# A hybrid decoder trunk on one core: weights split one unit less ahead in attention and the delta rule, and the norm factor of the last two heads applied without a pinned step

## The chip, the cores and the metric

The kernel runs on one core of a Trainium2 chip. The metric is device time in microseconds (us) of one execution. Five engines work side by side, each with a queue of its own that it goes through in order: PE (TensorE, matmul), DVE (VectorE), ACT (ScalarE), POOL (GpSimd) and SP (SyncE, which issues nearly all DMAs here). An instruction that waits for a semaphore holds up everything behind it in its own queue.

## The reference

Two layers of a decoder block over 512 tokens of width 1024, all in float32:

```python
def hybrid_layer(x, ...):
    h = rmsnorm(x, pre_mix_g)
    proj = h @ w_in              # q|k|v|z|beta|decay of DeltaNet, q|k|v of attention, gates A|B
    y_a = deltanet_branch(...) @ w_up_dn      # causal conv + silu, gated delta rule, gated RMSNorm
    y_b = swa_sink_branch(...) @ w_up_sw      # sliding window attention with sinks
    mix = (sigmoid(gate_a) * y_a + sigmoid(gate_b) * y_b) @ w_o
    x = x + rmsnorm(mix, post_mix_g)
    h2 = rmsnorm(x, pre_mlp_g)
    ff = square(relu(h2 @ w_ff1)) @ w_ff2     # width 4096
    return x + rmsnorm(ff, post_mlp_g)

# end of deltanet_branch, o being the output of the delta rule:
    o = rmsnorm(o, norm_g) * silu(z)
```

The DeltaNet branch has 8 heads of 128. In each, with the decay g summed over the tokens of a chunk, a triangular matrix is inverted and the state passes from chunk to chunk. Attention has 16 query heads and 2 key heads of 64, blocks of 128 tokens, each block looking at itself and the one before. The norm of a head's output is one factor for each token: the RMSNorm over the head's 128 values.

## The kernel before

**Weights.** They lie in device memory as units of 128 x 1024 float32, in the order of use. `load` (L312) brings a unit into a tile `wr`, of which there are WR = 6. `prefetch` (L411) splits it: ACT copies it to `wh`, rounded to the matmul's fp32r type (L419), and DVE subtracts that from `wr` to get the remainder `wl` (L420). There are LOOK = 4 tiles of each. The left operand is split the same way into a high and a low part, and a product is three matmuls: wh by high (L435), wh by low (L436), wl by high (L437). One unit is 24 matmuls of 128 x 512. `weights` (L424) hands out unit i, and calls `prefetch(i + LOOK)` first: at the place in the program where unit i is used, the splits of all units up to i + 3 have been written.

**Order.** The kernel is written as a trace in program order. The tile framework then puts each engine's instructions in order by that place in the program and by what is ready when, so a line that is written later may come later in its queue, or may not. Two things pin an order by hand: `Order` ties all instructions of an engine that are traced between `begin` and `end` to the order of the trace, and `tc.keep_in_program_order` ties one instruction behind the one that its engine was given before it.

**Stages of a layer.** First the norm, keys and values of attention, and its queries, 8 units, stored to a scratch area `qd`. Then attention: a loop of 16 passes (L1124 to L1146). The list MIX gives each pass projections of the shared input h: K is `k_unit` (a DeltaNet head's keys, their triangle `uu`, stored to `ud`), G is `gb_unit` (a part of gate B), A is `ga_early` (a part of gate A). Each pass also starts one attention group (t, g, e): block t, key head g, one parity e of the query heads.

- `att_q` loads a group's queries `qT` through SP (L1032), one pass ahead.
- `att_group` makes the scores `ps_s` on PE (L1055), the masked scores `M`, their maximum `nm` and the sinks' part `es` on DVE, the exponentials and the normalisation on ACT (L1073, L1079); a pass or two later PE transposes them to `ps_pt`, and they are split into a high and a low part `pf`; POOL makes a masked copy `pc` of each (L1095); PE multiplies by the values into `ps_o` (L1102). `att_prep`, once per block, also makes the block's keys `kT_h` on ACT (L1024).
- The decay of DeltaNet's heads 4 to 7 comes in the same loop, in `k_unit` (that of heads 0 to 3 beside the attention queries): `decay_load` brings a tile `D` from `gd` through SP (L817), `decay_of` masks it on POOL (L821), ACT takes its last column's exponential `egl` (L823) and four exponentials of the tile (L825), and it is stored to `dd`. Its four buffers (T[5]) are shared with `uu` and others in turn, so a load of D waits until what stood there has been read for the last time, by the store to `ud` for instance.

Then V, Q and Z of the first head, the 8 units of attention's up-projection, beside which `solve` inverts the triangles on DVE, and the delta rule over 8 heads: `d_dense` (V, Q and Z projections of the next head), `d_inverse`, `d_chain` (the state from chunk to chunk), and the output's norm in `d_tail`. The last gate units `ga_unit` follow, then `yT` (the heads' outputs, split), DeltaNet's up-projection, the merge with the gates, the out projection and the MLP.

**`d_tail`** (L1292) is a generator that `d_step` moves on by one step: the sum of squares goes to memory (`sd`); it comes back as `ff`, POOL raises it to -1/2 and stores it to `fd`; `fb` is loaded from there, spread over the partitions (L1307); and DVE multiplies the head's output `yf` by it (L1309), pinned in program order. A `yield` stands between the steps, so each one is written at another place in the program: for heads 5, 6 and 7 between the gate units (L1419) and behind them (L1420).

Of the kernel before, what the change touches and what calls it, by code (L numbers as in the profile page):

```python
# [15 lines left out]
ALU = mybir.AluOpType  # L16
# [9 lines left out]
H = 8  # L26
# [17 lines left out]
LOOK = 4  # L44
# [99 lines left out]
def hybrid_trunk(ctx, tc, x, positions, pre_mix_g, dn_conv_w, dn_a_log, dn_dt_bias, dn_norm_g,  # L144
                 sw_sinks, post_mix_g, pre_mlp_g, post_mlp_g, wpk, out, depth=2, dump=None):
    nc = tc.nc
    x = x.rearrange("b s d -> (b s) d")
    out = out.rearrange("b s d -> (b s) d")
# [12 lines left out]
    tt, ts = nc.vector.tensor_tensor, nc.vector.tensor_scalar  # L161
# [21 lines left out]
    def PS(name):  # L183
        return pp.tile([P, 512], F32, name=name, tag="ps")
# [127 lines left out]
    def load(key):  # L312

        wr = wp.tile([P, 1024], F32, name="wr", bufs=WR)
        w = width(key[4])
        dma(wr[:, :w], wpk[index[key], :, :w])
        return wr

    def width(n_):
        return 512 if n_ < 0 else n_ if n_ > 512 else 2 * n_ if n_ else 1024  # L320

    def blocks(a, n_):
        k = 4 if n_ < 0 else n_ // NB if n_ > 512 else 2 if n_ else 8
        return a[:, :width(n_)].rearrange("p (k c) -> p k c", k=k)
# [82 lines left out]
            specs.append((tuple(key), key[4]))  # L407
    pre = []
    used = [0]

    def prefetch(n, wr=None, sub=tt):  # L411
        while len(pre) < min(n, len(specs)):
            src, n_ = specs[len(pre)]
            if wr is None:
                wr = src() if callable(src) else load(src)
            wh = wp.tile([P, 1024], F32R, name="wh", bufs=LOOK)
            wl = wp.tile([P, 1024], F32R, name="wl", bufs=LOOK)
            w = width(n_)
            nc.scalar.copy(wh[:, :w], wr[:, :w])  # L419
            sub(out=wl[:, :w], in0=wr[:, :w], in1=wh[:, :w].bitcast(F32), op=ALU.subtract)  # L420
            pre.append((blocks(wh, n_), blocks(wl, n_)))
            wr = None

    def weights():  # L424
        i = used[0]
        used[0] += 1
        prefetch(i + LOOK)
        r, pre[i] = pre[i], None
        return r

    def mm_a(ps, aT, ks=range(KT), w=None):
        wh, wl = w = w or weights()
        for k in ks:
            hi, lo = aT[k]
            mm(ps, lhsT=wh[:, k, :], rhs=hi, start=k == 0, stop=False)  # L435
            mm(ps, lhsT=wh[:, k, :], rhs=lo, start=False, stop=False)  # L436
            mm(ps, lhsT=wl[:, k, :], rhs=hi, start=False, stop=k == KT - 1)  # L437
        return w
# [54 lines left out]
    def mm_b4(pss, aT, then=lambda: None, onto=False):  # L493

        for j in range(4):
            if j == 2:
                then()
            wh, wl = weights()
            for t in range(NT):
                tsl = slice(t * P, (t + 1) * P)  # L500
                for r in range(2):
                    hi, lo = aT[j * 2 + r]
                    k = j * 2 + r
                    mm(pss[t], lhsT=hi[:, tsl], rhs=wh[:, r, :], start=k == 0 and not onto, stop=False,  # L504
                       skip_group_check=onto)
                    mm(pss[t], lhsT=hi[:, tsl], rhs=wl[:, r, :], start=False, stop=False,  # L506
                       skip_group_check=onto)
                    mm(pss[t], lhsT=lo[:, tsl], rhs=wh[:, r, :], start=False, stop=k == KT - 1,  # L508
                       skip_group_check=onto)

    def mm_c(pss, left, onto=False, js=range(2)):

        for j in js:
            wh, wl = weights()
            hi, lo = left[j]
            for t in range(2):
                for r in range(2):
                    c = slice(r * 256 + t * P, r * 256 + (t + 1) * P)
                    first, last = j + r == 0 and not onto, j + r == 2
                    mm(pss[t], lhsT=hi[:, c], rhs=wh[:, r, :], start=first, stop=False,  # L520
                       skip_group_check=onto)
                    mm(pss[t], lhsT=hi[:, c], rhs=wl[:, r, :], start=False, stop=False,
                       skip_group_check=onto)
                    mm(pss[t], lhsT=lo[:, c], rhs=wh[:, r, :], start=False, stop=last,
                       skip_group_check=onto)
# [14 lines left out]
    def split(src, hi, lo, sign=1.0):  # L540
        if sign < 0:
            act(out=hi, in_=src, func=AF.Copy, scale=-1.0)
            stt(out=lo, in0=src, scalar=-1.0, in1=hi.bitcast(F32), op0=ALU.mult, op1=ALU.subtract)
            return
        nc.scalar.copy(hi, src)
        tt(out=lo, in0=src, in1=hi.bitcast(F32), op=ALU.subtract)  # L546

    def pair(U, name):
        return U(name + "_h", F32R), U(name + "_l", F32R)
# [100 lines left out]
    for l in range(depth):  # L650
# [68 lines left out]
        else:  # L719
# [16 lines left out]
            mm_a2(qf0, hT, 1, wq0)  # L736
            order.end()

        cwr = T[6]("cwr")
        dma(cwr[:96, :P], dn_conv_w[l].rearrange("k (m p) -> (k m) p", p=P))  # L740
        ps = PS("ps_cw")
# [26 lines left out]
        for t in range(NT):  # L768
# [11 lines left out]
           in1=dtb.unsqueeze(2).broadcast_to([P, H, NC]), op=ALU.add)  # L780
# [509 lines left out]
        def d_tail(h):  # L1290

            w, y1 = dn.pop(("t", h))  # L1292
            wh, wl = pair(T[5], "w")
            split(w, wh, wl)
            ps = PS("ps_w")
            mm(ps, lhsT=ones_r, rhs=wh, start=True, stop=False)
            mm(ps, lhsT=ones_r, rhs=wl, start=False, stop=True)
            nc.scalar.copy(w[0:1], ps[0:1])
            dma(sd[h:h + 1, :], w[0:1])
            yield  # L1300
            ff = sm.tile([P, NC], F32, name="ff")
            dma(ff, sd[h, :].rearrange("(p j) -> p j", p=P))
            ptt(out=ff, in0=ff, in1=mhalf, op=ALU.pow)
            pdma(fd[h, :].rearrange("(p j) -> p j", p=P), ff)
            yield
            fb = T[6]("fb")
            dma(fb, fd[h, :].partition_broadcast(P))  # L1307
            yield
            tc.keep_in_program_order(tt(out=y1, in0=y1, in1=fb, op=ALU.mult))  # L1309

        tails = [d_tail(h) for h in range(H)]

        def d_step(*hs):
            for h in hs:
                if 0 <= h < H:
                    next(tails[h], None)
# [100 lines left out]
        for m in range(NA2, KT):  # L1417
            ga_unit(m)
            d_step(H - 1, H - 2, H - 3)  # L1419
        d_step(H - 1)  # L1420
        yT = []
        for k in range(KT):
            p_ = pair(T[4 + k % 4], "yT")
# [360 lines left out]
```

## Time and profile before

| | |
|---|---|
| median of 3 runs | 1816.69 us (1814.89 to 1816.76) |
| the profiled execution | 1817.76 us around a span of 1816.1 us |
| TensorE clock granted in it | 0.998 |
| DMA | 294.33 MB, mean 162 GB/s |
| chain that ended last | PE 80%, DVE 8%, ACT 6%, DMA 3%, issue 2%, POOL 1% |
| costliest groups | split of weights: ACT `wh` 372.7 us in 366, DVE `wl` 435.4 us in 366 |

The span runs from the first instruction to the last in one execution on the chip, as the hardware profiler saw it; the execution's own time holds 1.66 us more. Busy times of engines are sums over the span. In the rows of the timeline the first column is the time from the start of the span in us, the second how long the instruction was at work, then the engine, the line, the operation and its tiles, how many alike were put together (x4), and in brackets how long the engine had waited just ahead of it and for whom. In the rows of the waits stand the waiting instruction, whom it waited for, the sum in us, the count and the mean. An SPq row is SP handing a DMA to its queue: the data land later. Lines are those of the kernel before; the two layers are the same program, so that each place in layer 0 has a twin in layer 1, 896.5 us later.

### The profile page before, as it was taken

Reading aid. Unit: us, or ns where it says so; the run is one execution under the profiler, and the core shown is the slowest. Engines: PE = TensorE matmul, PEld = TensorE weight load, DVE = VectorE, ACT = ScalarE, POOL = GpSimd, SP = SyncE. Lnnn points to the kernel's source line nnn. Section 1 sums busy time; section 2 is a strip of 40 time slices with the busy share of each in tenths; the row PEclk is TensorE's granted clock in tenths of the full one; section 3 lists DMA queues with packets and bytes.
Section 4 is the critical chain, followed back from the end, with each engine's and each line's share of the span. In section 5 each row is a group of like instructions: output and inputs, shape, how many; then the busy total and the mean of one; then the engine's idle time right before and its main releaser. Section 6 shows DMA issues by size and latency. Waiting matters only on the chain.

```text
span 1816.1 us, 28412 instructions
## 1 busy us (share of the span) xinstructions
PE 1787.7 (98%) x10220; PEld 1511.2 (83%) x10220; DVE 1376.8 (76%) x2576; ACT 998.8 (55%) x2039; POOL 200.3 (11%) x346
## 2 busy tenths in 40 slices
PE   9999999999999999999999999999999999999998
PEld 7887878887788888989888877888877888889896
DVE  6489796888666878888565897878884669698973
ACT  7578732444434656566555887234443347566572
POOL 2013202221101000000020131022111010000000
PEclk9999999999999999999999999999999999999999
DMA  6845447555453255554557453575554533555551
GB/s 221 276 142 184 117 139 232 169 163 152 128 190 135 82 163 153 173 179 147 185 182 239 156 169 105 170 231 162 159 139 148 167 116 104 175 164 161 174 178 55
DMA packets 167071, 294.33 MB, mean 162 GB/s; under 512 B 34497, under 2 KB 83969, under 8 KB 166930
## 3 DMA queue, kind: packets, MB, share of 16 engines
q1 hardware_dynamic: 166418, 292.48, 51.9%
q8 instruction: 80, 1.31, 0.3%
q14 instruction: 61, 0.50, 0.1%
q0 software_dynamic: 512, 0.03, 0.0%
HBM read 246.19 MB, written 46.27 MB: 161 GB/s over the span
## 4 chain that ended last, share of the span: by engine, by line
PE 80%; DVE 8%; ACT 6%; DMA 3%; issue 2%; POOL 1%; SPq 0%; DVEq 0%; POOLq 0%; ACTq 0%
PE ps_f L435 2%; PE ps_f L436 2%; PE ps_f L437 2%; PE ps_zp L435 2%; PE ps_zp L436 2%; PE ps_b L506 2%; PE ps_us L436 2%; PE ps_b L504 2%; PE ps_b L508 2%; PE ps_us L437 2%; PE ps_us L435 2%; PE ps_zp L437 2%; PE ps_ud L436 1%; PE ps_qp L435 1%; PE ps_qp L436 1%
## 5 line engine op out<-in xcount | busy, mean ns | idle before, releaser
L419 ACT CAST wh<-wr 128x1024 fp32r<-128x1024 f32 (+2 forms) x366 | 372.7, 1023 | 416.1 <-PE ps_us L436 62.7
L420 DVE TENSOR_TENSOR wl<-wr,wh 128x1024 fp32r<-128x1024 f32 (+2 forms) x366 | 435.4, 1196 | 170.3 <-ACT wh L419 164.4
L571 POOL TENSOR_TENSOR pr<-pq,pw 128x1 f32<-128x1 f32 x16 | 9.8, 615 | 787.6 <-DVE pq L570 787.6
L435 PE MATMUL ps_f<-g_h,wh 128*128 128x512 f32 x160 | 62.4, 390 | 0.0
L436 PE MATMUL ps_f<-g_l,wh 128*128 128x512 f32 x160 | 62.4, 390 | 0.0
L437 PE MATMUL ps_f<-g_h,wl 128*128 128x512 f32 x160 | 62.2, 389 | 0.0
L1073 ACT ACTIVATE M<-M,nm 128x128 f32<-128x128 f32 x128 | 49.8, 390 | 10.9 <-DVE nm L1068 10.8
L436 PE MATMUL ps_ud<-yT_l,wh 128*128 128x512 f32 x128 | 50.7, 396 | 2.9 <-DVE yT_l L546 2.9
L435 PE MATMUL ps_zp<-h_h,wh 128*128 128x512 f32 x128 | 50.5, 394 | 2.8 <-DVE vv L883 2.8
L436 PE MATMUL ps_qp<-h_l,wh 128*128 128x512 f32 x128 | 53.2, 415 | 0.0
L437 PE MATMUL ps_qp<-h_h,wl 128*128 128x512 f32 x128 | 53.1, 415 | 0.0
L435 PE MATMUL ps_vp<-h_h,wh 128*128 128x512 f32 x128 | 52.8, 413 | 0.0
L437 PE MATMUL ps_vp<-h_h,wl 128*128 128x512 f32 x128 | 52.6, 411 | 0.0
L435 PE MATMUL ps_qp<-h_h,wh 128*128 128x512 f32 x128 | 52.5, 410 | 0.0
L435 PE MATMUL ps_ga<-h_h,wh 128*128 128x512 f32 x128 | 51.4, 402 | 1.0 <-ACT sga L946 1.0
L378 DVE TENSOR_TENSOR wr<-wr 128x512 f32<-128x512 f32 x72 | 47.5, 685 | 6.0 <-DMA wr<-in_weights_dram 5.5
L435 PE MATMUL ps_kp<-h_h,wh 128*128 128x512 f32 x128 | 51.5, 403 | 0.0
L436 PE MATMUL ps_vp<-h_l,wh 128*128 128x512 f32 x128 | 51.2, 400 | 0.0
L435 PE MATMUL ps_gb<-h_h,wh 128*128 128x512 f32 x128 | 51.2, 400 | 0.0
L437 PE MATMUL ps_ga<-h_h,wl 128*128 128x512 f32 x128 | 50.5, 395 | 0.0
L437 PE MATMUL ps_ud<-yT_h,wl 128*128 128x512 f32 x128 | 50.5, 395 | 0.0
L436 PE MATMUL ps_ga<-h_l,wh 128*128 128x512 f32 x128 | 50.5, 394 | 0.0
(449 smaller groups left out, 5958.3 us busy)
## 6 DMA issues: line engine op xcount, KB each, us to landing
wr<-in_weights_dram SPq DMA_DIRECT2D x336, 512.0 KB, 3.7
qT<-qd SPq DMA_DIRECT2D x32, 256.0 KB, 3.5
D<-dd SPq DMA_DIRECT2D x24, 256.0 KB, 2.8
xd<-xo SPq DMA_DIRECT2D x12, 512.0 KB, 2.6
xt<-xd SPq DMA_DIRECT2D x24, 256.0 KB, 6.1
qd<-qf_h SPq DMA_DIRECT2D x16, 256.0 KB, 4.2
qd<-qf_l SPq DMA_DIRECT2D x16, 256.0 KB, 3.4
D<-gd SPq DMA_DIRECT2D x16, 256.0 KB, 4.2
```

Of the source, the lines that this page charges most:

```text
L378: tt(out=o_, in0=i0, in1=i1, op=ALU.add)
L419: nc.scalar.copy(wh[:, :w], wr[:, :w])
L420: sub(out=wl[:, :w], in0=wr[:, :w], in1=wh[:, :w].bitcast(F32), op=ALU.subtract)
L435: mm(ps, lhsT=wh[:, k, :], rhs=hi, start=k == 0, stop=False)
L436: mm(ps, lhsT=wh[:, k, :], rhs=lo, start=False, stop=False)
L437: mm(ps, lhsT=wl[:, k, :], rhs=hi, start=False, stop=k == KT - 1)
L504: mm(pss[t], lhsT=hi[:, tsl], rhs=wh[:, r, :], start=k == 0 and not onto, stop=False, skip_group_check=onto)
L506: mm(pss[t], lhsT=hi[:, tsl], rhs=wl[:, r, :], start=False, stop=False, skip_group_check=onto)
L508: mm(pss[t], lhsT=lo[:, tsl], rhs=wh[:, r, :], start=False, stop=k == KT - 1, skip_group_check=onto)
L571: ptt(out=r, in0=q1, in1=mhalf[:, 0:1], op=ALU.pow)
L1073: act(out=M[:, j * P:(j + 1) * P], in_=M[:, j * P:(j + 1) * P], func=AF.Exp, bias=nm[:, j:j + 1], accum_out=den[:, j:j + 1])
```

## The change

There are two parts.

Between the end of the first attention query projection and the end of the delta rule of each layer, `weights` now calls `prefetch(i + 3)` where it called `prefetch(i + 4)`: at the place where unit i is used, splits up to unit i + 2 have been written. From `yT` on it is 4 again. The number of buffers stays: 6 `wr`, 4 `wh`, 4 `wl`. No split, load or matmul is added or dropped.

In `d_tail`, for heads 6 and 7 alone, the `yield` between the load of `fb` and the multiplication goes, and so does the pin: the multiplication is written in the same step as the load, one step earlier, and its place in DVE's queue is left to the framework.

```diff
@@ -407,6 +407,7 @@
     pre = []
     used = [0]
+    ahead = [LOOK]
 
@@ -424,7 +425,7 @@
     def weights():
         i = used[0]
         used[0] += 1
-        prefetch(i + LOOK)
+        prefetch(i + ahead[0])
         r, pre[i] = pre[i], None
         return r
 
@@ -736,6 +737,7 @@
             mm_a2(qf0, hT, 1, wq0)
             order.end()
 
+        ahead[0] = LOOK - 1
         cwr = T[6]("cwr")
@@ -1305,8 +1307,11 @@
             yield
             fb = T[6]("fb")
             dma(fb, fd[h, :].partition_broadcast(P))
-            yield
-            tc.keep_in_program_order(tt(out=y1, in0=y1, in1=fb, op=ALU.mult))
+            if h < H - 2:
+                yield
+            m_ = tt(out=y1, in0=y1, in1=fb, op=ALU.mult)
+            if h < H - 2:
+                tc.keep_in_program_order(m_)
 
@@ -1418,6 +1423,7 @@
             ga_unit(m)
             d_step(H - 1, H - 2, H - 3)
         d_step(H - 1)
+        ahead[0] = LOOK
         yT = []
```

The change writes lines in another order, so each engine's queue may come out otherwise. Rows of these queues stand in the prediction, before and after: the operation's line, its kind, its tiles as out<-in with a running number for each tile, and its shape. In after the lines behind the diff's first hunk are 1 to 6 higher, and the running numbers of tiles are shifted by a few, which means nothing.

## The prediction

> **What bounds the kernel now.** I read the page first, then the busy time of each engine by stretch, then who waited for whom inside the stretches that the change touches, then the timeline of those places, engine by engine.
>
> ```profile
> span 1816.1 us, 28412 instructions
> PE 1787.7 (98%) x10220; PEld 1511.2 (83%) x10220; DVE 1376.8 (76%) x2576; ACT 998.8 (55%) x2039; POOL 200.3 (11%) x346
> ```
>
> PE is busy 98% of the span, so an edit that adds or removes no matmul can only win back time in which PE stands still: 1816.1 - 1787.7 = 28.4 us in all, a little more where a pause is hidden by the overlap of neighbouring matmuls. What the change can reach is less. Its queues differ from before's only inside attention and in a few DVE rows after it (shown below), so I ask for attention's share:
>
> ```profile
> 130.00:193.00 63.00, 60.44 (x321) 49.77 (x320) 57.93 (x177) 53.82 (x169) 21.12 (x25) 1.00 0.55 167
> 1026.50:1089.50 63.00, 60.44 (x321) 49.75 (x320) 57.76 (x177) 53.70 (x169) 21.15 (x25) 1.00 0.54 168
> ```
>
> The columns are the stretch, its length, then PE, PEld, DVE, ACT and POOL busy. The first row is layer 0, the second its twin in layer 1, 896.5 us later. PE idles 63.00 - 60.44 = 2.56 us in each, while DVE is at 92% and ACT at 85%: here the two vector engines set the pace at places. Which waits these are:
>
> ```profile
> PE ps_o L1102 <- POOL pc L1095: 1.9, 3, 0.8
> PE ps_s L1055 <- ACT kT_h L1024: 0.5, 1, 0.5
> ...
> ACT egl L823 <- POOL D L821: 3.0, 2, 1.9
> ```
>
> PE waits three times for POOL's masked copy of the probabilities (pc) and once for ACT's keys (kT_h); ACT in turn stands 3.0 us for POOL, which is waiting for the decay tile D.
>
> **The change part by part.** *The norm factor of heads 6 and 7.* The end of a layer on DVE, before and then after (yf is a head's output, fb its factor, yT_l the split, wl a weight split):
>
> ```order
> L420 TENSOR_TENSOR wl_5602<-wr_5599,wh_5601 128x1024
> L1309 TENSOR_TENSOR yf_5208<-yf_5208,fb_5527 128x512
> L546 TENSOR_TENSOR yT_l_5575<-yf_4166,yT_h_5574 128x512
> L1309 TENSOR_TENSOR yf_5428<-yf_5428,fb_5562 128x512
> L546 TENSOR_TENSOR yT_l_5591<-yf_5208,yT_h_5590 128x512
> ```
>
> ```order
> L421 TENSOR_TENSOR wl_5602<-wr_5599,wh_5601 128x1024
> L1312 TENSOR_TENSOR yf_5202<-yf_5202,fb_5521 128x512
> L547 TENSOR_TENSOR yT_l_5569<-yf_4160,yT_h_5568 128x512
> L1312 TENSOR_TENSOR yf_5422<-yf_5422,fb_5557 128x512
> L547 TENSOR_TENSOR yT_l_5585<-yf_5202,yT_h_5584 128x512
> ```
>
> Nothing moved: the pin is gone, but each row stands where it stood. I cost this edit at 0, and the wait that it is about stays:
>
> ```profile
> 497.43 0.50 PE L436 MATMUL ps_ud<-yT_l,wh 128*128 128x512 f32 x1 [0.85 <-DVE yT_l L546]
> ```
>
> *Weights split one unit less ahead.* No split is dropped; each is written later in the program. In the delta rule every queue keeps its order, so it costs 0 there. In attention the splits fall behind work that was ready. At layer 0, before and then after, on DVE (nm, es and den are softmax scalars of a group, uu the delta rule's triangle, wl the unit that PE needs two units on):
>
> ```order
> L1067 TENSOR_REDUCE nm_1821<-M_1806 128x4
> L420 TENSOR_TENSOR wl_1863<-wr_1860,wh_1862 128x1024
> L1068 TENSOR_TENSOR nm_1821<-nm_1821,nsk_411 128x4
> L914 SCALAR_TENSOR_TENSOR uu_1897,ssk_1898<-ps_a_1892,ident_75 128x128
> L1070 TENSOR_TENSOR es_1824<-nm_1821,nsk_411 128x4
> ```
>
> ```order
> L1069 TENSOR_REDUCE nm_1815<-M_1800 128x4
> L916 SCALAR_TENSOR_TENSOR uu_1891,ssk_1892<-ps_a_1886,ident_75 128x128
> L1070 TENSOR_TENSOR nm_1815<-nm_1815,nsk_411 128x4
> L916 SCALAR_TENSOR_TENSOR uu_1891,ssk_1892<-ps_a_1886,ident_75 128x128
> L1072 TENSOR_TENSOR es_1818<-nm_1815,nsk_411 128x4
> L916 SCALAR_TENSOR_TENSOR uu_1891,ssk_1892<-ps_a_1886,ident_75 128x128 x2
> L1065 COPY_PREDICATED M_1909<-ge_86,ps_s_1910 128x256
> L918 TENSOR_SCALAR ssk_1892<-ssk_1892 128x4
> L421 TENSOR_TENSOR wl_1968<-wr_1965,wh_1967 128x1024
> ```
>
> The split went from ahead of the softmax's maximum to behind it. A second effect is on SP, which issues the loads (ud is the triangle's store, qT a group's queries, D the decay tile), before and then after:
>
> ```order
> L928 DMA ud_104<-uu_1772 128x4x128
> L1032 DMA qT_2205<-qd_101 128x4x128
> L817 DMA D_1968<-gd_110 128x512
> L817 DMA D_2080<-gd_110 128x512
> L316 DMA wr_2474<-in_weights_dram 128x1024
> ```
>
> ```order
> L930 DMA ud_104<-uu_1766 128x4x128
> L819 DMA D_1962<-gd_110 128x512
> L819 DMA D_2074<-gd_110 128x512
> L1034 DMA qT_2199<-qd_101 128x4x128
> L316 DMA wr_2501<-in_weights_dram 128x1024
> ```
>
> Both D loads now go ahead of qT, which waits for PE; for the pair before this one only the first D load does. POOL follows: it masks D ahead of pc. I take the places in turn.
>
> *Place 1, the first pair.* Rows of SP, POOL, ACT, DVE and PE:
>
> ```profile
> 130.35 0.37 SPq L928 DMA_DIRECT2D ud<-uu  x1
> 131.90 0.37 SPq L1032 DMA_DIRECT2D qT<-qd  x1
> 132.32 0.98 SPq L817 DMA_DIRECT2D D<-gd  x2
> ```
>
> ```profile
> 136.75 0.63 POOL L821 TENSOR_SCALAR_AFFINE_SELECT D<-D 128x512 f32<-128x512 f32 x1 [0.47 <-POOL pc L1095]
> 138.40 0.64 POOL L821 TENSOR_SCALAR_AFFINE_SELECT D<-D 128x512 f32<-128x512 f32 x1 [1.02 <-DMA D<-gd]
> 138.98 1.69 POOL L1095 TENSOR_SCALAR_AFFINE_SELECT pc<-pf_l 128x512 fp32r<-128x512 f32 x1
> ```
>
> ```profile
> 135.03 1.28 ACT L1079 ACTIVATE M<-M,den 128x128 f32<-128x128 f32 x4
> 137.41 0.21 ACT L823 ACTIVATE egl<-D 128x4 f32<-128x4 f32 x1 [1.10 <-POOL D L821]
> ```
>
> ```profile
> 131.50 1.22 DVE L420 TENSOR_TENSOR wl<-wr,wh 128x1024 fp32r<-128x1024 f32 x1
> ...
> 137.91 0.68 DVE L546 TENSOR_TENSOR pf_l<-ps_pt,pf_h 128x512 fp32r<-128x512 f32 x1
> ...
> 138.97 1.21 DVE L420 TENSOR_TENSOR wl<-wr,wh 128x1024 fp32r<-128x1024 f32 x1
> ```
>
> ```profile
> 139.28 0.40 PE L1102 MATMUL ps_o<-pf_l,vp 128*128 128x512 f32 x1
> 139.52 0.39 PE L1102 MATMUL ps_o<-pc,vp 128*128 128x512 f32 x1
> 140.73 0.50 PE L1102 MATMUL ps_o<-pc,vp 128*128 128x512 f32 x1 [0.82 <-POOL pc L1095]
> ```
>
> PE would have begun the last matmul at 139.52 + 0.24 = 139.76, so it lost 0.97. Now the first D load issues at about 130.8 instead of 132.32, the second about 0.6 earlier; masked D is there by 135.9 and 138.3. On DVE the 0.3 to 0.4 us of gaps between the moved rows close, so pf_l ends near 138.2 instead of 138.59. The other split (138.97 now) follows at once, and pc meets it again: today pc ends at 140.67, 0.49 after that split (140.18). Split 138.2 to 139.4, pc done 139.9: about 0.75 of the 0.97 is won. The bounds are 0.4 (pc slips as today) and 0.97.
>
> The Trainium skill, "SBUF — State Buffer", section "SBUF: two separate sides", says that a DVE instruction with two SBUF inputs and a reading GpSimd instruction take one shared port pair in turn, the first to start holding it for its whole length. By that rule a pc that starts first would end after 0.64 and place 1 would win all of its 0.97; the trace agrees on the exclusion (0.64 alone, 1.69 beside a split), not on who goes first, so I stay with the rows.
>
> *Place 2, the keys.* PE then waits for kT_h, made by ACT at the end of an almost gapless chain:
>
> ```profile
> 153.81 0.26 ACT L1024 CAST kT_h<-ps_k 64x128 fp32r<-64x128 f32 x1
> ```
>
> ```profile
> 154.12 0.50 PE L1055 MATMUL ps_s<-kT_h,qT 128*128 128x256 f32 x2 [0.52 <-ACT kT_h L1024]
> ```
>
> So PE keeps of place 1 only what ACT gains. ACT now has D's exponentials ahead of the normalisation (the row at 135.03). It is free at 135.14 and goes on at 135.9, a wait of 0.8 instead of 1.10 and some 0.2 of small ones. **Places 1 and 2 together: 0.6** per layer, between 0.3 and 1.0.
>
> *Place 3, the second pair.*
>
> ```profile
> ud<-uu SPq DMA_DIRECT2D x7, 256.0 KB, 3.1
> D<-gd SPq DMA_DIRECT2D x4, 256.0 KB, 4.2
> ```
>
> ```profile
> 156.75 0.46 SPq L928 DMA_DIRECT2D ud<-uu  x1
> ...
> 159.93 0.97 SPq L817 DMA_DIRECT2D D<-gd  x2
> ```
>
> ```profile
> 164.41 0.64 POOL L821 TENSOR_SCALAR_AFFINE_SELECT D<-D 128x512 f32<-128x512 f32 x1 [1.75 <-DMA D<-gd]
> 165.00 2.29 POOL L1095 TENSOR_SCALAR_AFFINE_SELECT pc<-pf_h 128x512 fp32r<-128x512 f32 x1
> 167.25 0.75 POOL L821 TENSOR_SCALAR_AFFINE_SELECT D<-D 128x512 f32<-128x512 f32 x1
> 167.96 0.63 POOL L1095 TENSOR_SCALAR_AFFINE_SELECT pc<-pf_l 128x512 fp32r<-128x512 f32 x1
> ```
>
> ```profile
> 165.59 1.21 DVE L420 TENSOR_TENSOR wl<-wr,wh 128x1024 fp32r<-128x1024 f32 x1
> ```
>
> ```profile
> 168.03 0.21 ACT L823 ACTIVATE egl<-D 128x4 f32<-128x4 f32 x1 [1.87 <-POOL D L821]
> ```
>
> ```profile
> 167.59 0.39 PE L1102 MATMUL ps_o<-pc,vp 128*128 128x512 f32 x1
> 168.64 0.50 PE L1102 MATMUL ps_o<-pc,vp 128*128 128x512 f32 x1 [0.67 <-POOL pc L1095]
> ```
>
> PE lost 168.64 - (167.59 + 0.23) = 0.82. All is 0.6 earlier by now, so the first D load issues behind ud at 156.6 instead of 159.93 and lands at 160.8. The second overwrites what that store reads and waits for its 3.1 us: issued at 159.3, landed at 163.5, masked at 164.2. Both pc follow: pf_h's by 164.9, pf_l's 0.5 after the split, that is at 164.9 + 1.21 + 0.5 = 166.6. PE asks for it at 167.82 - 0.6 = 167.2. The wait goes; if the first pc also slips behind the split, both are done at 167.2, still in time. **0.75**, between 0.3 and 0.82.
>
> *Place 4.* ACT's 1.87 us wait above goes too, so ACT reaches the next head's keys (kk) some 3 us earlier, and PE's pause for them ends:
>
> ```profile
> 184.30 0.71 PE L909 MATMUL ps_a<-kk 128*128 128x128 f32 x4 [0.15 <-DVE uu L926]
> ```
>
> The matmul ahead began at 183.67; against the usual 0.23 PE lost 0.4. **0.4**, between 0.2 and 0.4.
>
> *What hides the later splits.* The split at 131.50 is of the unit that PE begins here:
>
> ```profile
> 150.16 0.47 PE L435 MATMUL ps_gb<-h_h,wh 128*128 128x512 f32 x1
> ```
>
> It was done 17.4 us ahead, and moves by about 2 us. The furthest move (ACT's wh row 18 places back) is some 4 to 7 us against a like lead. Without that cover a late split would cost its full 1.2 us and the cast's 1.05.
>
> **Sum:** 0.6 + 0.75 + 0.4 = 1.75 us per layer, 3.5 us for two, to be carried to the end. The profiled execution took 1817.76 us around its 1816.1 us span, 1.07 above the median of 1816.69. So 1814.3 for its like, and **1813.2** against the median; with every term at its bound, 0.9 to 2.2 per layer, 1815 down to 1812.3.
>
> **The rivals.** *Taken back later.* Behind attention PE waits again:
>
> ```profile
> 239.16 0.47 PE L435 MATMUL ps_zp<-h_h,wh 128*128 128x512 f32 x1 [1.38 <-DVE vv L883]
> ```
>
> If the work in front of vv on DVE does not start earlier, this wait grows by what was won and 0 to 1.5 us remains: 1816. Against it: order there is unchanged and its inputs come from PE and from the same triangle stores.
> *More than that.* If the vector engines keep the lead that PE can't use (ACT is 3 us ahead at place 4), the 1.38 goes as well: 1.75 + 1.38 = 3.1 per layer, 1810.4.
> *It does nothing.* The moved rows sit beside a PE that is 98% busy, and if landings swallow the earlier issue the time stays at 1816.7.
> *Slower.* ACT's normalisation now stands behind D. It ends 0.21 + 3 x 0.3 + 1.28 = 2.4 us after POOL has masked D, and PE's transposes want it at 139.9 or so. From a masked D at 137.5 on, every us late is lost: the load would have to take 5.9 instead of 4.2. To lose 1.8 us per layer after the other terms are paid, it would have to take over 9: 1820.5.
>
> **How the numbers follow.** About 0.2%, 3.6 us, is what a measurement of this kernel can tell from no change. Forecast 0.60, half of it beyond that bound because 3.5 lies on it; more 0.08; taken back 0.12; nothing 0.12; slower 0.08. So faster 0.30 + 0.08 = 0.38, same 0.30 + 0.12 + 0.12 = 0.54, slower 0.08. The range runs from the second rival's time, 1810.4, to 0.6 above the median, 1817.3, and leaves out the slower case and half of "more".
>
> **What would show it.** Right: ACT's wait for POOL D falls from 3.0 to about 1 us, PE's wait for pc from 1.9 to about 0.7, and the stretch from the triangle of head 3 to the first ga unit shortens by 1.7 us in each layer. Wrong: kT_h later than before, pc still ending with 167.9 or later in its stretch, or a wait for vv longer by what was won. The waits at 497.43 and its twin should be as before but for how the fb load happens to land.

## The result, and the profile after

The changed kernel takes 1811.24 us (median of 9 runs, 1810.59 to 1812.44), the kernel before 1814.96 us beside it (9 runs, 1814.21 to 1820.31). The ratio is 0.9974, with a 95% interval of 0.9964 to 0.9985: faster by 3.7 us, clearly more than no change. Before's median over nine runs is 1.7 us below that of the three that the forecast started from, so the difference is what compares: 3.5 us were forecast, 3.7 measured.

The profiled execution took 1810.75 us around its span. Its page, the span and the engines:

```profile
span 1809.0 us, 28408 instructions
PE 1785.0 (99%) x10220; PEld 1510.7 (84%) x10220; DVE 1371.6 (76%) x2576; ACT 997.9 (55%) x2039; POOL 204.7 (11%) x346
```

The two profiled executions differ by 7.1 us in their spans, twice the medians' difference. Taking the same matmul in both traces and subtracting the starts shows where: 0.7 us in the first 12 us, where the queues are the same, 4.6 in the two attention stages, and on balance 1.8 at the ends of the delta rule, where layer 0 loses 0.66 and layer 1 gains 2.44. The first and the last are chance: e1, which has the change's queues, gains nothing in the first 12 us, and the waits at a layer's end scatter in the runs below. One profile of each kernel does not tell an effect of this size from the span. The stretches of attention tell more (stretch, length, then PE, PEld, DVE, ACT, POOL busy):

```profile
130.00:193.00 63.00, 61.87 (x328) 51.60 (x327) 57.40 (x180) 54.12 (x172) 22.25 (x25) 1.00 0.56 172
1026.50:1089.50 63.00, 62.18 (x324) 51.65 (x323) 56.44 (x177) 54.48 (x176) 22.18 (x25) 1.00 0.58 174
```

PE's idle time fell from 2.56 us to 1.13 and 0.82. What PE gained is more than this fall (2.19 and 2.42 us, below), in part because a matmul is shown 0.39 us long at a distance of 0.23, so that the first 0.16 us of a pause counts as busy. Who waited for whom in the first stretch:

```profile
ACT egl L825 <- POOL D L823: 1.0, 2, 0.6
PE ps_s L1057 <- ACT kT_h L1026: 0.7, 2, 0.5
PE ps_o L1104 <- POOL pc L1097: 0.4, 1, 0.4
```

ACT's wait for the decay tile went from 3.0 to 1.0, PE's for the masked copy pc from 1.9 to 0.4. PE's for the keys kT_h did not go away; it grew from 0.5 to 0.7.

By the same subtraction, and without the 0.70 us that after is ahead from its start, layer 0 gains 1.12 at place 1 (with the keys of place 2), 0.99 at place 3 and 0.07 from there to the end of attention: 2.19 us. Layer 1 gains 1.41, 0.96 and 0.03, with rounding 2.42.

*Place 1 after*, on SP and POOL:

```profile
129.65 0.37 SPq L930 DMA_DIRECT2D ud<-uu  x1
130.07 0.50 SPq L819 DMA_DIRECT2D D<-gd  x1
131.20 0.37 SPq L1034 DMA_DIRECT2D qT<-qd  x1
```

```profile
134.41 0.64 POOL L823 TENSOR_SCALAR_AFFINE_SELECT D<-D 128x512 f32<-128x512 f32 x1 [0.87 <-DMA D<-gd]
...
137.46 1.56 POOL L1097 TENSOR_SCALAR_AFFINE_SELECT pc<-pf_l 128x512 fp32r<-128x512 f32 x1 [1.00 <-DVE pf_l L547]
```

The store ud is issued where it was (130.35 before, less 0.70), but D's load now follows at once and not 1.97 us later; D is masked 1.6 us sooner. The second pc starts 0.8 us sooner. It still meets a split (DVE at 137.31) and takes 1.56 us, yet it is done at 139.02, where before was done at 140.67: 0.95 us sooner beyond the 0.70. PE's row at this place shows no wait any more:

```profile
138.82 0.75 PE L1104 MATMUL ps_o<-pc,vp 128*128 128x512 f32 x2
```

*Place 2 after*, the keys, on ACT and PE:

```profile
151.98 0.26 ACT L1026 CAST kT_h<-ps_k 64x128 fp32r<-64x128 f32 x1
```

```profile
152.29 0.51 PE L1057 MATMUL ps_s<-kT_h,qT 128*128 128x256 f32 x2 [0.52 <-ACT kT_h L1026]
```

PE waits for them as long as before, but both have moved 1.13 us (153.81 to 151.98, less 0.70).

*Place 3 after*, POOL and PE:

```profile
162.46 0.64 POOL L823 TENSOR_SCALAR_AFFINE_SELECT D<-D 128x512 f32<-128x512 f32 x1 [1.46 <-DMA D<-gd]
163.05 1.70 POOL L1097 TENSOR_SCALAR_AFFINE_SELECT pc<-pf_h 128x512 fp32r<-128x512 f32 x1
164.70 0.63 POOL L1097 TENSOR_SCALAR_AFFINE_SELECT pc<-pf_l 128x512 fp32r<-128x512 f32 x1
```

```profile
165.75 0.62 PE L1104 MATMUL ps_o<-pc,vp 128*128 128x512 f32 x2
```

Both masks are done before either pc, and the second pc ends at 165.33, ahead of PE's asking. *Place 4 after*: the pause for kk is gone (PE is 0.42 us further ahead there), but 6 us later a new one stands, for the next block's keys, and takes most of it back:

```profile
186.85 0.39 PE L1057 MATMUL ps_s<-kT_h,qT 128*128 128x256 f32 x1 [0.21 <-ACT kT_h L1026]
```

### The profile page after: what moved, and what is told of

It is laid out like the page before. It is cut to its first block, busy times and chain, and to the rows that moved or that the text cites. A ratio compares the mean times of both kernels' runs of the same rounds, so it can differ in the third digit from the quotient of the medians.

```text
span 1809.0 us, 28408 instructions
## 1 busy us (share of the span) xinstructions
PE 1785.0 (99%) x10220; PEld 1510.7 (84%) x10220; DVE 1371.6 (76%) x2576; ACT 997.9 (55%) x2039; POOL 204.7 (11%) x346
## 3 DMA queue, kind: packets, MB, share of 16 engines
q8 instruction: 80, 1.31, 0.3%
## 4 chain that ended last, share of the span: by engine, by line
PE 80%; DVE 8%; ACT 6%; DMA 3%; issue 2%; POOL 1%; SPq 0%; DVEq 0%; POOLq 0%; ACTq 0%
PE ps_f L437 2%; PE ps_f L436 2%; PE ps_f L438 2%; PE ps_zp L436 2%; PE ps_zp L437 2%; PE ps_b L507 2%; PE ps_us L436 2%; PE ps_b L509 2%; PE ps_b L505 2%; PE ps_us L438 2%; PE ps_us L437 2%; PE ps_zp L438 2%; PE ps_qp L436 1%; PE ps_qp L437 1%; PE ps_qp L438 1%
## 5 line engine op out<-in xcount | busy, mean ns | idle before, releaser
L437 PE MATMUL ps_zp<-h_l,wh 128*128 128x512 f32 x128 | 50.3, 393 | 0.0
```

## The experiments

Theory A: the whole effect is in attention, made by the first part of the change; A1 puts it on the decay tile's earlier loads, A2 on the DVE order itself. The rivals: B, the norm factor's step has a share; C, the lower lookahead acts beyond attention; D, a slow store scatters the end of each layer.

For each run the table gives the ratio to the kernel before, timed beside it, and what PE gained over each layer's attention against before's profile.

| run | ratio, 95% interval | attention, layer 0 and 1 (us) |
|---|---|---|
| the change | 0.9974 (0.9964 to 0.9985) | -2.19, -2.42 |
| e1, first part alone | 0.9968 (0.9957 to 0.9978) | -2.27, -2.52 |
| e2, second part alone | 1.0001 (0.9992 to 1.0010) | -0.34, -0.95 |
| e3, D's loads first | 0.9978 (0.9969 to 0.9987) | -1.87, -1.87 |
| e4, and their masks first | 0.9985 (0.9975 to 0.9994) | -2.05, -2.38 |
| e5, three splits held back | 0.9980 (0.9971 to 0.9989) | -1.69, -1.68 |
| e6, lookahead behind attention | 0.9997 (0.9988 to 1.0007) | +0.13, +0.21 |
| e7, the change and values first | 0.9954 (0.9942 to 0.9967) | -2.35, -2.37 |
| e8, the change, factor stored by ACT | 1.0025 (1.0016 to 1.0034) | -2.27, -2.19 |

In attention, before, e2 and e6 have the same queues; their sums over two layers (0, -1.29, +0.34) average -0.3. The change, e1, e7 and e8 have the same queues there too (e7 and e8 differ further on): -4.61, -4.79, -4.72 and -4.46, on average -4.6. So attention gives 4.3 us, with about 1 us of scatter in one profile of the old order. The timed intervals of the change (2.7 to 6.5 us) and of e1 (4.0 to 7.8) hold that.

### The two parts apart: e1 and e2

e1 keeps the first part and takes the second back:

```diff
-            if h < H - 2:
-                yield
-            m_ = tt(out=y1, in0=y1, in1=fb, op=ALU.mult)
-            if h < H - 2:
-                tc.keep_in_program_order(m_)
+            yield
+            tc.keep_in_program_order(tt(out=y1, in0=y1, in1=fb, op=ALU.mult))
```

> The first part of the change alone (weights one unit less ahead), the norm factor as before. Theory A (the gain is all in attention, made by the first part): the same time as the whole change, ratio 0.9975 within 0.001, and PE's place in its program shifts by -2.0 to -2.5 us over each attention stage (130 to 193 us and its twin). Theory B (part of the gain comes from the norm factor at the end of a layer): only about half of it, 0.9985 to 0.9992, with attention still giving its -4.4 us.

e2 is the kernel before with these lines the other way round, and nothing else.

> The second part alone (norm factor of heads 6 and 7 unpinned and one step earlier), splits as before. Theory A: no row of any queue stands elsewhere, so ratio 1.000 within 0.001 and no step in attention; the waits for yT_l come out anywhere between 0.5 and 2.5 us, as the load of the factor lands. Theory B: ratio 0.998 to 0.999, with the wait for yT_l shorter in both layers.

e1 has all of the change's gain, e2 none. B falls. That e2's profile is 0.34 and 0.95 us ahead in attention, where no step was expected, is scatter, since every row of its queues stands where it does in before. The wait for yT_l at the end of a layer, in before's profile and in that of e2:

```profile
PE ps_ud L436 <- DVE yT_l L546: 2.9, 2, 2.1
```

```profile
PE ps_ud L436 <- DVE yT_l L546: 0.9, 2, 0.6
```

The queues are the same, the waits 2.9 and 0.9 us. So the wait scatters, and neither the change nor e2 moved the order of rows that lies behind it. PE does not wait there for the output of head 6 or 7, whose factors are late, but for the low half of head 5, the sixth yT_l of the layer. In before's layer 0 its high half, cast on ACT, was there at 491.98, and the row itself ran at 496.69:

```profile
491.37 0.61 ACT L545 CAST yT_h<-yf 128x512 fp32r<-128x512 f32 x1
```

```profile
496.08 0.69 DVE L1309 TENSOR_TENSOR yf<-yf,fb 128x512 f32<-128x512 f32 x1 [3.84 <-DMA fb<-fd]
496.69 0.68 DVE L546 TENSOR_TENSOR yT_l<-yf,yT_h 128x512 fp32r<-128x512 f32 x1
```

In DVE's queue the multiplication by head 6's factor stands ahead of head 5's split, before and after alike, and DVE stood 3.84 us for that factor. With the two rows the other way round the split could have run in that pause; no run here tries it.

And a long wait costs more than itself. Here is before's layer 1 from that wait on (PE's granted clock is the third last number):

```profile
1390.00:1395.00 5.00, 3.18 (x15) 2.29 (x13) 1.10 (x2) 0.37 (x1) 0.81 (x1) 1.00 0.58 153
1395.00:1400.00 5.00, 4.75 (x14) 3.78 (x15) 0.20 (x1) 0.24 (x1) 1.07 (x2) 0.66 0.58 222
```

```profile
1395.74 0.63 PE L437 MATMUL ps_ud<-yT_h,wl 128*128 128x512 f32 x1
1396.17 0.63 PE L435 MATMUL ps_ud<-yT_h,wh 128*128 128x512 f32 x1
...
1398.73 0.43 PE L435 MATMUL ps_ud<-yT_h,wh 128*128 128x512 f32 x1
```

After 2.07 us of idling the granted clock is lower, and the eight matmuls from 1395.25 to 1398.73 take 0.43 us each in place of 0.23: 1.6 us on top of the wait. In the change the wait at this place is shorter, and the matmuls behind it start at their usual distance; that makes the 2.44 us between the two profiles (1.0 of wait, the rest of clock; 1389.99 is the same matmul as 1395.25):

```profile
1389.99 0.50 PE L437 MATMUL ps_ud<-yT_l,wh 128*128 128x512 f32 x1 [1.10 <-DVE yT_l L547]
1390.32 0.40 PE L438 MATMUL ps_ud<-yT_h,wl 128*128 128x512 f32 x1
1390.56 0.39 PE L436 MATMUL ps_ud<-yT_h,wh 128*128 128x512 f32 x1
```

### What in attention wins: e3 and e4

e3 is the kernel before, with one kind of edge added: on SP, qT of a group may not go ahead of D's load of a head.

```diff
+AHEAD = {4: 10, 6: 13, 7: 13}
...
 def decay_load(h):
-            dma(c4(d), gd[h * NC:(h + 1) * NC, :].partition_broadcast(P))
+            i_ = dma(c4(d), gd[h * NC:(h + 1) * NC, :].partition_broadcast(P))
+            if h in AHEAD:
+                dloads.setdefault(AHEAD[h], []).append(i_)
...
 def att_q(t, g, e):
-            dma(c4(a.bitcast(F32)), qgroups[:, g, :, e, t * P:(t + 1) * P])
+            i_ = dma(c4(a.bitcast(F32)), qgroups[:, g, :, e, t * P:(t + 1) * P])
+            for d_ in dloads.get(t * 4 + g * 2 + e, ()):
+                behind(i_, d_)
```

AHEAD gives for each head the group. `behind` adds a NoSync edge, which orders two instructions of one queue. DVE, ACT, POOL and PE keep before's order row by row; SP's differs in three loads per layer.

> Before, with nothing moved but SP's loads of the decay tile D: D of head 4 goes ahead of qT of group 10, D of heads 6 and 7 ahead of qT of group 13, as in the change. All splits, and DVE, ACT, POOL and PE rows stay as before. Theory A1 (what wins is D arriving earlier): POOL's waits for D and ACT's for POOL shrink, PE's waits for pc go at the second pair (0.8) and at least half at the first (0.5 to 1.0): -1.2 to -1.9 us per layer, ratio 0.998 to 0.9987. Theory A2 (what wins is that the softmax and the triangle on DVE stand ahead of the splits): D's arrival alone gives less than 0.4 per layer, ratio 0.9996 to 1.000.

e4 adds to e3, on POOL, an edge that puts the masks of D for heads 4 and 7 ahead of the pc of groups 4 and 7 (MASK = {4: 4, 7: 7}, in the same manner).

> As the run with D's loads first, and on POOL the masks of D for heads 4 and 7 ahead of the masked copies pc, as in the change: SP's and POOL's queues in attention as after, DVE, ACT and PE as before. Theory A1: as the run before it or better, up to the whole of the change's attention, -1.5 to -2.3 us per layer, ratio 0.9975 to 0.9984. Theory A2: under 0.4 per layer, or worse than before where pc now stands behind a mask that waits for D.

Three loads in another place, and no split moved, win 1.87 us of the 2.2 to 2.4 per layer. A1 holds for most of it. The step of place 3 is whole (0.99 and 0.96); that of place 1, with the keys of place 2, is 0.79 and 0.82 against 1.12 and 1.41. PE still waits for pc there:

```profile
138.94 0.50 PE L1116 MATMUL ps_o<-pc,vp 128*128 128x512 f32 x1 [0.46 <-POOL pc L1109]
```

pf_l, from which pc is copied, ended at 138.59 in before. In the change it ends at 137.38, 0.5 us sooner beyond the 0.70, as DVE's rows ahead of it were put otherwise:

```profile
136.70 0.68 DVE L547 TENSOR_TENSOR pf_l<-ps_pt,pf_h 128x512 fp32r<-128x512 f32 x1
```

That much DVE's order does (A2). But it does not decide the rest of 0.3 to 0.55 us per layer, because PE waits for the keys some 12 us later. In e4 no row of DVE moved either. In its layer 0 PE waits 0.59 us for the same pc, longer than in e3, and yet behind the keys it is 0.93 us ahead of before, in layer 1 1.31. e4's attention lacks 0.14 and 0.04 us of the change's, which is less than the scatter of one profile. A share of A2 is therefore not shown; most of what e3 lacks can be POOL's order, or chance. e4's time is no better than e3's: its ratio is just above the 0.9975 to 0.9984 that A1 gave for it, and its profile has a wait of 3.4 us at the end of layer 1:

```profile
PE ps_ud L445 <- DVE yT_l L555: 4.4, 2, 3.4
```

### Why one unit less does that: e5 and e6

e5 is the kernel before with three splits of each layer held back on DVE by hand, the lookahead at 4. LATE gives the row (tile and head or group) and the unit whose split goes behind it:

```diff
+LATE = {("cj", 3): 21, ("ssk", 5): 24, ("es", 10): 26}
...
+    def late_split(l, kind, n, a):
+        if (kind, n) in LATE:
+            u = LATE[kind, n] + 183 * l
+            if u in wls:
+                behind(wls[u], a)
+            due[u] = a
```

> Before, with only three splits per layer held back on DVE: units 21, 24 and 26 of each layer behind the triangle's scalars of heads 3 and 5 and behind group 10's es, about where the change has them. The framework then plans the rest of attention anew, and puts SP's loads of D ahead of qT as in the change. Theory A (what wins is where the splits and with them D's loads stand in attention, nothing else): the same as the whole change, -2.0 to -2.5 us per attention stage, ratio 0.997 to 0.998. Theory C (the change's lower lookahead does something beyond these rows, in the delta rule or through the buffers): at most half of it, 0.9985 or more.

Three splits of the 183 in a layer suffice for the framework to put D's loads first too, and bring 0.998 in time. Attention's -1.7 is less than I expected: the rows around came out slightly otherwise than in the change. So the link between splits and loads is the framework's planning. Why it then puts the loads there is not shown; it may reckon with the triangle, its store and D's free buffer sooner, once a split of 1.2 us no longer stands ahead of them. On the chip the store at place 1 goes out no sooner; only the order behind it changes.

e6 sets the lower lookahead behind attention alone:

```diff
+        ahead[0] = LOOK - 1
         dn = {}
```

> One unit less ahead only behind attention (solve, up-projection of attention, delta rule); attention as before. Two splits per layer move in DVE's queue. Theory A: nothing, ratio 1.000 within 0.001, no step at attention or in the 40 us behind it. Theory C: 0.9985 or less.

1.000 within its interval, and no step: C falls, the delta rule neither wins nor loses.

### A better version, and one that is not: e7 and e8

Behind attention PE waits 1.4 us in each layer for the first head's values, in before and after alike. e7 writes their projection ahead of the splits of attention's last block:

```diff
-        for t in range(NT):
+        def o_split(t):
             tsl = slice(t * P, (t + 1) * P)
...
+        for t in range(NT - 1):
+            o_split(t)
         turn0 = d_dense(0, lambda: steps(2))
+        o_split(NT - 1)
```

> The changed kernel, with the convolution of head 0's values (vv) written ahead of the splits of attention's last block (oT): on DVE its three steps go ahead of 4 of the last oT_l splits. PE's wait for vv, 1.4 us per layer in before and after alike, should fall by those splits' 0.2 us each and the gap, to 0.5 to 0.9: -0.5 to -0.9 per layer, ratio to before 0.9960 to 0.9968 where the change alone is at 0.9968 to 0.9974. Rival: oT, which the up-projection needs some 8 us later, becomes late, and PE waits there for what it won.

```profile
235.53 0.47 PE L436 MATMUL ps_zp<-h_h,wh 128*128 128x512 f32 x1 [0.52 <-DVE vv L885]
```

The wait is 0.52, PE is 0.86 us further ahead behind it in both layers, and no wait for oT takes it back. The edit also moved rows further on, 60 of PE's between 309 and 327 us and their twins, where PE gains another 0.2 us or so. This is the fastest version here: 1807.98 us, 0.9954 of before, a little below the forecast 0.9960 to 0.9968, against 0.9968 and 0.9974 for the change's queues. The intervals overlap; it is the step behind vv in the trace that shows the gain.

e8 issues the factor's store from ACT:

```diff
-            pdma(fd[h, :].rearrange("(p j) -> p j", p=P), ff)
+            nc.scalar.dma_start(fd[h, :].rearrange("(p j) -> p j", p=P), ff)
```

> The changed kernel, with the store of the norm factor (fd) issued by ACT in place of POOL. In the profiles so far the load of the factor (fb) of head 6 is issued 3.1 us (after), 6.0 (before) and 7.3 (D's loads first on SP and POOL) behind the start of that store's issue, and PE's wait for yT_l follows it (1.1, 2.1, 3.4 in layer 1). Theory D (the software queue's landing time is what scatters the runs): fb goes out 2 to 3 us after, both waits for yT_l under 1 us, the spread of the runs narrower, ratio to before 0.9960 to 0.9970. Rival: ACT stands waiting for POOL's ff and delays what is behind it in the delta rule: slower than the change by 1 us or more.

The rival came true. The store of head 7 stands in ACT's queue ahead of the yT_h of heads 5 and 6, and waits for POOL's ff:

```profile
495.16 0.33 ACTq L1306 DMA_DIRECT2D fd<-ff  x1
495.53 1.14 ACT L546 CAST yT_h<-yf 128x512 fp32r<-128x512 f32 x2 [6.08 <-POOL ff L1305]
```

ACT stood 6.08 us, and PE waited 5.9 us over both layers, with the lower clock behind both waits:

```profile
PE ps_ud L436 <- ACT yT_h L546: 5.9, 2, 3.4
```

For head 6 in layer 0 the way from the store's issue to the load's (485.83 to 490.02, 4.2 us) was not shorter than POOL's in the change either (484.87 to 488.16, 3.3 us), so theory D's cure fails; what makes this way vary from 2.9 (e5) to 7.3 us (e4) with POOL stays open.

## Why the prediction was right in the mechanism and wrong in its weight

- *The norm factor costs and wins nothing*: right. Its rows stood where they stood, and e2 is at 1.0001.
- *Queues that differ only inside attention and in a few DVE rows after it*: not quite. Four rows of ACT and three loads of SP also changed places at 58 to 66 us, beside the attention queries, and in their twins. PE shows no step there in after's trace, so nothing hangs on it.
- *No effect in the delta rule*: right (e6).
- *The mechanism in attention*: right. D's loads ahead of qT, masks and pc sooner, PE's waits for pc gone at places 1 and 3. e3 shows most of it with the loads alone.
- *Places 1 and 2, "0.6 per layer, between 0.3 and 1.0"*: too small, and outside its own bounds: 1.12 and 1.41. That "PE keeps of place 1 only what ACT gains" held; the term that failed is ACT's gain, put at 0.3 for the wait and 0.2 for small ones (0.5, which then stands as 0.6). ACT gained 1.13 in layer 0 and 1.39 in layer 1. In before's layer 0 it idled 20.07 - 18.42 = 1.65 us from 134.00 to the end of the keys at 154.07, after 18.94 - 18.12 = 0.82 us on the same way:

```profile
134.00:154.07 20.07, 18.38 (x90) 14.38 (x88) 18.30 (x50) 18.42 (x56) 8.39 (x9) 1.00 0.56 171
```

```profile
133.30:152.24 18.94, 18.07 (x90) 14.37 (x88) 16.57 (x47) 18.12 (x56) 7.54 (x9) 1.00 0.58 182
```

  The rows of the two stretches are 0.83 of idle and 0.30 of busy time apart. Of the idle time 0.46 is the wait for D (1.10 to 0.64) and 0.21 the wait for den, which vanished. In layer 1 the wait for D fell by 0.98 (1.39 to 0.41).
- *Place 3, 0.75, between 0.3 and 0.82*: 0.99 and 0.96; the whole wait went and a little more, where I had taken something off.
- *Place 4, 0.4*: right where it was forecast (0.42), and then taken back by the next block's keys; 0.07 and 0.03 remained. The rival "taken back" did happen, though in attention, not at vv, where the wait is 1.4 us as before.
- *The sum*, 3.5 us: 4.3 to 4.6 in attention by the profiles, 3.7 by the medians. The size was fair, with some luck: places 1 and 2 were 0.5 to 0.8 us per layer too small, place 3 0.2 too small and place 4 0.35 too large. The lower bounds add up to 0.8 and not 0.9, and a loss of 1.8 per layer gives 1820.3 and not 1820.5; neither changes the forecast.
- *The weight*: this is the step that failed, "half of it beyond that bound because 3.5 lies on it". With it "same" got 0.54 and "faster" 0.38, and the kernel became measurably faster, by 0.26%. Two things were wrong in it. The bound was too wide: 3.6 us was taken as what a measurement can tell from no change, but the interval of nine runs of each kernel reaches 1.9 us to either side, so 3.5 us would have been told as well. And the sum that was laid against it was too small, by the terms above: 0.6 for places 1 and 2 where 1.12 and 1.41 came. Both terms that carry the sum had been taken below the waits that the rows showed (0.97 and 0.82), while nothing in the profile spoke for a loss beside them. All three waits at their whole size would have given 2.2 per layer, 4.4 us, clear of the bound. That 2.2 and 2.4 also came is luck in part, since place 4's 0.4 was taken back and places 1 and 2 gave more than 0.97. Two of the three terms were taken smaller for caution and the chances then lowered once more, which is the same doubt counted twice.

On pc and the split the Trainium skill, "SBUF — State Buffer", section "SBUF: two separate sides", said that the one which starts first holds a shared port pair for its whole length. The change's trace has both orders. At 163.05 a split had begun just ahead (163.04) and pc took 1.70 us, above. Here pc (POOL at 229.14, 0.64 us) began first, and the split behind it is the one that is long, 1.65 in place of 1.21 us:

```profile
229.20 1.65 DVE L421 TENSOR_TENSOR wl<-wr,wh 128x1024 fp32r<-128x1024 f32 x1
```

These rows agree with the rule. Before's row at 165.00, shown in the prediction, does not: there pc began 0.59 us ahead of the split (165.59), and yet the split took its usual 1.21 us and pc 2.29. What decides in that case stays open. At place 1 the split still went first, by 0.15 us, and pc came 0.95 us sooner for other reasons: pf_l ended 0.51 sooner, POOL no longer had a mask of D in front of pc when pf_l was there (0.31), and pc took 0.13 less.

## What to carry to other kernels

Where a planner orders the queues, a change of one kind of instruction can win through another: compare the queues row by row, DMA queues first, since a load that stands behind another load which waits for PE is late by all of that wait. When the profile shows whom the busy engine waits for, and the change makes that cause come sooner by more than the wait, count the whole wait, then look for the next engine in line. And for effects of 0.2%, take the difference stage by stage from several profiles: spans differ by as much from chance.

## What was not expected of the hardware

- The way of a 2 KB factor through memory (store from POOL, then the load of it) took 2.9 to 7.3 us between two issues for head 6 in profiles with the same rows there, and the load itself 3.2 to 5.7 us from its issue to the multiplication. PE's waits behind it came to 0.9 to 4.4 us per execution over both layers, as much as the whole change brings. The same store from ACT was no quicker (4.2 and 4.6 us).
- PE's clock fell after short waits: 2.07 us (before), 3.42 (e4), 2.55 and 3.39 (e8) were followed by matmuls of 0.43 us in place of 0.23, one of 2.11 us (e7) was not, and none of the other fifteen waits at this place, up to 1.15 us, nor of the eighteen of 1.37 to 1.43 us for vv was. Behind e8's wait of 3.39 us the clock fell five matmuls late. The Trainium skill, "TensorE: Matmul & The Clock Gate", section "Part 1: The HAM clock gate (the "warmup" mystery)", has the clock halved after at least one idle window of about 3.4 us, and windows that run freely. Half the rate for about 3.4 us (1395.25 to 1398.73) agrees with the trace; that 2.07 us of idling suffices does not.
- The wait for pc in attention also scatters: with the old queues PE gained 0.95 us in layer 1's attention in one profile (e2) and lost 0.21 in another (e6).
